# Products of a scan's keys: from two quarters of the PE array and one bank to four quarters and two banks

## The chip, the cores and the metric

The kernel runs on one core of a Trainium2 chip. The metric is the device time of one execution in microseconds (us). The engines are TensorE (PE in the rows; PEld is its weight load), VectorE (DVE), ScalarE (ACT), GpSimd (POOL) and SyncE (SP). SP only issues DMAs here; ScalarE issues DMAs too, in the same order as its other work. A quarter of the array is a 64x64 part of TensorE's 128x128 array: its rows are the partitions that the operands lie on, its columns the partitions of PSUM that the result goes to.

## The reference, cut to what matters

One layer of a diffusion backbone: a modulated input is projected to the columns of eight attention heads and of eight RWKV-7 heads with two directions; both go through an output projection, a norm and an MLP. What the change touches belongs to the RWKV-7 heads. The reference runs them as a recurrence:

```python
s_kk = jnp.einsum('bhij,bhj->bhi', S, kk_t)
S = (S * w_t[:, :, None, :] - s_kk[..., None] * (kk_t * a_t)[:, :, None, :]
     + v_t[..., None] * k_t[:, :, None, :])
return S, jnp.einsum('bhij,bhj->bhi', S, r_t)
```

The kernel computes it in chunks of 64 tokens. For each chunk, head and direction it needs a 64x64 matrix of products of decayed keys, which it then inverts as a triangular system.

## The kernel before, in words

The kernel has a first phase (`phase1`, to about 1000 us) and a second (`tail`). The first phase takes the 2304 tokens in three blocks of 768. For each block it projects the tokens to 27 groups of 128 columns (`project`, L450: 24 matmuls into a PSUM bank of the pool `psM`, which has two, emptied by ScalarE in L453). Between the halves of each projection `side` hands out one step of the other work, the scan terms among it.

The scan terms are made by `r1a` and `r1b`, 36 times each: three blocks, four pairs of heads (`p`), three groups of four chunks (`t`). `r1a` computes the decayed keys: `ar` and `bk`, two buffers each. They hold two heads on the halves of the 128 partitions, both directions (`d`), four chunks (`c`) and two kinds of vectors. The tile `ei` of `r1a` (written by the exponential in L646) has one buffer, which it shares, by its tag, with `lab` of `r1b`.

`r1b` stores `ar` and `bk` by SP's queue (L676 to L679). It then forms the key products (L686) for both heads, both directions and four chunks: 16 products of 64x64 by 64x64, all into one bank, `psl`, from the pool `psC`, which has two. ScalarE copies the bank to `lab` in one instruction (L688) and issues two stores to the DRAM tensor LB, one for each direction (L690). For all but the context tokens a matmul with a matrix of ones follows, the bonus sum (L693), into another bank of `psC`, which VectorE empties (L695). The pool `psC` also serves the transposes of values (L726) and of the inputs (L415).

Later `solve` reads LB back, inverts the matrices on VectorE (L760, L761) and joins the parts by 32x32 matmuls (L800). In the second phase the chunks are chained; there L1141 and L1145 form products of keys for each chunk with 64x64 weights, in two banks.

The program is written in the order of these calls, with a priority that falls in that order. A planner with its own model of times then orders the instructions of each engine: an instruction that is not ready by that model lets later ones go ahead, so that a burst of L686 stands within the matmuls of a projection. It also picks the buffers and puts in the semaphores. On the chip each engine keeps the planned order.

Of the kernel before, what the change touches and what calls it, by code (L numbers as in the profile page):

```python
# [8 lines left out]
F32 = mybir.dt.float32  # L9
# [52 lines left out]
class Kern:  # L62
# [604 lines left out]
    def r1b(self, sb, p, t, v, cell):  # L667
        nc = self.nc
        R = self.r1
        ctx = sb == 0 and t == 0  # L670
        s = slice(t * 256, t * 256 + 256)
        c0 = sb * 12 + t * 4
        ar, bk = cell["ar"], cell["bk"]
        w = 64 if ctx else 128
        for d in range(2):
            nc.sync.dma_start(self.AR[:, d, c0:c0 + 4, p, 0:w], ar[:, d].rearrange("p c x t -> p c (x t)")[:, :, 0:w])  # L676
            nc.sync.dma_start(self.BK[0:64, d, c0:c0 + 4, p, :], bk[0:64, d].rearrange("p c x t -> p c (x t)"))
            for x in range(2):
                nc.sync.dma_start(self.BK[64:128, d, c0:c0 + 4, p, (1 - x) * 64:(2 - x) * 64], bk[64:128, d, :, x, :])  # L679
        psl = self.psC.tile([128, 512], F32, name="psc")  # L680
        for d in range(2):
            for c in range(4):
                for hd in range(2):
                    hs = slice(hd * 64, hd * 64 + 64)
                    o = (d * 4 + c) * 64
                    nc.tensor.matmul(psl[hs, o:o + 64], lhsT=bk[hs, d, c, 0, :], rhs=ar[hs, d, c, 0, :], start=True, stop=True)  # L686
        lab = R.tile([128, 2, 4, 64], F32, tag="ei", name="lab")
        nc.scalar.copy(lab.rearrange("p d c t -> p (d c t)"), psl)  # L688
        for d in range(2):
            nc.scalar.dma_start(self.LB[:, d, c0 * 4 + p:(c0 + 3) * 4 + p + 1:4, :], lab[:, d])  # L690
        if not ctx:
            psb = self.psC.tile([128, 512], F32, name="psc")
            nc.tensor.matmul(psb[:, :256], lhsT=self.bones, rhs=cell["kds"], start=True, stop=True)  # L693
            bon = R.tile([128, 256], F32, tag="q1", name="bon", bufs=3)
            nc.vector.tensor_tensor(bon, psb[:, :256], v[:, s], ALU.mult)  # L695
            g = sb * 768 + t * 256 - 256
            nc.sync.dma_start(self.BON[p, :, g:g + 256], bon)
# [1235 lines left out]
```

## Time and profile before

| what | value |
|---|---|
| median of 3 runs | 3413.09 us (3408.29 to 3415.94) |
| the profiled execution's own time | 3414.7 us |
| its span, first to last instruction | 3412.9 us |
| mean granted TensorE clock | 0.968 |
| TensorE busy | 3192.8 us (94%) |
| VectorE busy | 2599.1 us (76%) |
| ScalarE busy | 1523.7 us (45%) |
| chain of waits, share of TensorE | 65% |

Busy times are those of one profiled execution; instructions that issue DMAs or handle semaphores are not counted as busy. A matmul's end is modelled: consecutive matmuls overlap in the records, so that the time for which a burst holds TensorE is read from its first start to the start of what follows. Each product in 32-bit floats shows as two instructions.

### The profile page before, as it was taken

Reading aid. Unit: us, or ns where it says so; the run is one execution under the profiler, and the core shown is the slowest. Engines: PE = TensorE matmul, PEld = TensorE weight load, DVE = VectorE, ACT = ScalarE, POOL = GpSimd, SP = SyncE. Lnnn points to the kernel's source line nnn. Section 1 sums busy time; section 2 is a strip of 40 time slices with the busy share of each in tenths; the row PEclk is TensorE's granted clock in tenths of the full one; section 3 lists DMA queues with packets and bytes.
Section 4 is the critical chain, followed back from the end, with each engine's and each line's share of the span. In section 5 each row is a group of like instructions: output and inputs, shape, how many; then the busy total and the mean of one; then the engine's idle time right before and its main releaser. Section 6 shows DMA issues by size and latency. Waiting matters only on the chain.

```text
span 3412.9 us, 65231 instructions
## 1 busy us (share of the span) xinstructions
PE 3192.8 (94%) x25176; PEld 2602.5 (76%) x25176; DVE 2599.1 (76%) x4907; ACT 1523.7 (45%) x2891; POOL 511.0 (15%) x535
## 2 busy tenths in 40 slices
PE   7999899899988899899979989999999989999998
PEld 3888888889876677677667767777788868888886
DVE  5567977888788778767768878866766657899778
ACT  4555465456535455454432124343433343337333
POOL 0000000000005454545343321000000000010001
PEclk9999999999989999999989989999999989999999
DMA  7487366826675655455374546666644455445441
GB/s 259 119 244 213 95 170 167 223 71 178 174 201 145 144 140 126 122 133 128 101 199 150 175 152 224 210 198 206 210 150 148 145 206 162 154 161 203 146 160 69
DMA packets 765338, 561.67 MB, mean 165 GB/s; under 512 B 380412, under 2 KB 653564, under 8 KB 763620
## 3 DMA queue, kind: packets, MB, share of 16 engines
q1 hardware_dynamic: 691738, 523.14, 52.0%
q10 hardware_dynamic: 73290, 34.37, 3.5%
q8 instruction: 198, 3.24, 0.4%
q14 instruction: 112, 0.92, 0.1%
HBM read 359.70 MB, written 197.66 MB: 163 GB/s over the span
## 4 chain that ended last, share of the span: by engine, by line
PE 65%; DVE 14%; DMA 11%; SPq 3%; issue 3%; ACT 2%; POOL 1%; ACTq 0%; DVEq 0%; POOLq 0%
PE psm L450 14%; PE psa L1530 8%; PE psqb L1728 7%; PE psqa L1728 7%; PE psb L1530 4%; PE ops L1346 4%; PE pse L1530 2%; PE psv L1051 2%; DMA ks<-AR 1%; PE psm L468 1%; DMA w<-in_mlp_w 1%; PE pst L1022 1%; PE psg L1141 1%; PE psl L986 1%; PE psd L117 1%
## 5 line engine op out<-in xcount | busy, mean ns | idle before, releaser
L450 PE MATMUL psm<-xh,wh 128*128 128x386 f32 (+1 forms) x1104 | 378.4, 345 | 17.4 <-DVE xh L420 9.5
L450 PE MATMUL psm<-xl,wh 128*128 128x386 f32 (+1 forms) x1104 | 378.8, 343 | 3.1 <-DVE xl L421 3.1
L450 PE MATMUL psm<-xh,wl 128*128 128x386 f32 (+1 forms) x1104 | 376.6, 341 | 0.0
L450 PEld LDWEIGHTS psm<-xh,wh 128*128 128x128 f32 x1104 | 209.2, 190 | 44.8 <-ACT row L453 15.1
L450 PEld LDWEIGHTS psm<-xl,wh 128*128 128x128 f32 x1104 | 209.5, 190 | 16.0 <-issue 8.0
L450 PEld LDWEIGHTS psm<-xh,wl 128*128 128x128 f32 x1104 | 208.8, 189 | 6.1 <-issue 4.1
L1530 PE MATMUL psa<-xh,w1h 128*128 128x512 f32 x512 | 203.9, 399 | 5.1 <-DVE p L1556 4.6
L1794 POOL TENSOR_TENSOR acc<-acc,g 128x1024 f32<-128x1024 f32 x8 | 28.9, 3641 | 1178.2 <-DVE acc L1737 1178.2
L1530 PE MATMUL psa<-xh,w1l 128*128 128x512 f32 x512 | 201.7, 394 | 2.5 <-DVE w1l L1461 2.5
L1530 PE MATMUL psa<-xl,w1h 128*128 128x512 f32 x512 | 202.3, 395 | 0.0
L1678 ACT CAST ah<-al 128x1024 fp32r<-128x1024 f32 x98 | 103.0, 1051 | 213.2 <-DMA al<-HU 205.1
L760 DVE TENSOR_TENSOR stmp<-mp,xp 128x1 f32<-128x1 f32 (+30 forms) x310 | 175.4, 566 | 22.7 <-DMA mp<-LB 10.3
L1679 DVE TENSOR_TENSOR al<-al,ah 128x1024 fp32r<-128x1024 f32 x98 | 121.3, 1237 | 86.0 <-ACT ah L1678 85.9
L436 DVE TENSOR_TENSOR wl<-wst,wh 128x1024 fp32r<-128x1024 f32 x81 | 98.8, 1220 | 98.5 <-ACT wh L435 85.8
L1461 ACT CAST w1h<-w1s 128x512 fp32r<-128x512 f32 x96 | 59.6, 621 | 226.4 <-DVE w1s L1450 87.4
L1728 PE MATMUL psqa<-uh,ah 128*128 128x512 f32 x400 | 155.8, 393 | 3.7 <-ACT uh L1634 3.2
L1728 PE MATMUL psqa<-ul,ah 128*128 128x512 f32 x400 | 157.4, 394 | 0.0
L1728 PE MATMUL psqa<-uh,al 128*128 128x512 f32 x400 | 157.0, 392 | 0.0
L1728 PE MATMUL psqb<-uh,ah 128*128 128x512 f32 x384 | 149.7, 393 | 7.5 <-ACT uh L1634 7.5
L761 DVE TENSOR_REDUCE xp<-stmp 128x1 f32<-128x1 f32 (+30 forms) x310 | 153.9, 497 | 3.1
L1728 PE MATMUL psqb<-ul,ah 128*128 128x512 f32 x384 | 151.0, 393 | 0.0
L1728 PE MATMUL psqb<-uh,al 128*128 128x512 f32 x384 | 150.6, 392 | 0.0
(393 smaller groups left out, 8816.2 us busy)
## 6 DMA issues: line engine op xcount, KB each, us to landing
al<-HU SPq DMA_DIRECT2D x106, 512.0 KB
wst<-in_w_in SPq DMA_DIRECT2D x81, 512.0 KB
w<-in_mlp_w SPq DMA_DIRECT2D x32, 1024.0 KB
wp<-in_mlp_w SPq DMA_DIRECT2D x32, 1024.0 KB
wmod<-in_w_mod SPq DMA_DIRECT2D x48, 512.0 KB
HU<-p SPq DMA_DIRECT2D x96, 256.0 KB
HU<-s SPq DMA_DIRECT2D x84, 256.0 KB
bkc<-BK SPq DMA_DIRECT2D x36, 512.0 KB
```

Of the source, the lines that this page charges most:

```text
L117: self.nc.tensor.matmul(acc[32 * j:32 * j + n, :], lhsT=self.sil[:, k, 0:n], rhs=w, start=(k == 0), stop=(k == 7))
L436: nc.vector.tensor_tensor(wl, w, f32(wh), ALU.subtract)
L450: nc.tensor.matmul(ps[:, :y - x], lhsT=s[:, k, :], rhs=m[:, k, x:y], start=(i == 0), stop=(i == 23))
L760: nc.vector.tensor_tensor(tv, mp[:, i:i + 1, lo:lo + n].to_broadcast([128, n, n]), xp[:, lo:lo + n, lo:lo + n], ALU.mult)
L761: nc.vector.tensor_reduce(xp[:, lo:lo + n, i], tv, AX.X, ALU.add)
L1051: nc.tensor.matmul(cell["ps"][hs, i0:i0 + n, :], lhsT=vt[:, hs], rhs=x, start=first, stop=last, skip_group_check=True)
L1346: nc.tensor.matmul(ps, lhsT=x[:, k, :], rhs=w[:, k, c], start=(i == 0), stop=(i == 23))
L1461: made[n] = nc.scalar.copy(h, x).ins, V.tensor_tensor(l, x, f32(h), ALU.subtract).ins
L1530: nc.tensor.matmul(ps, lhsT=w[:, k, :], rhs=x[:, k, :], start=(i == 0 and pr in (1, 5, 2)), stop=(i == 11), skip_group_check=True)
L1678: fs += [lambda: nc.scalar.copy(ah, f32(al)), fb[0], lambda: V.tensor_tensor(al, f32(al), f32(ah), ALU.subtract), fb[1]]
L1679: lambda: V.tensor_tensor(al, f32(al), f32(ah), ALU.subtract), fb[1]]
L1728: nc.tensor.matmul(ps, lhsT=x[:, c, s], rhs=y[:, c, :], start=(i == 0 and new), stop=(i == 5 and end), skip_group_check=True)
```

## The change

The 16 products of a call go to two banks, one for each direction. In direction 0 a head's result goes to the same half of the partitions as its operands; in direction 1 it goes to the other half. The loop over chunks is now outermost. ScalarE copies each bank by itself. Direction 0 is stored by one DMA; direction 1, whose halves lie swapped, by two, each of 64 partitions. LB holds the same as before.

```diff
-        psl = self.psC.tile([128, 512], F32, name="psc")
+        psl = [self.psC.tile([128, 4, 64], F32, name="psc") for _ in range(2)]
+        hs = [slice(0, 64), slice(64, 128)]
+        for c in range(4):
+            for d in range(2):
+                for h in range(2):
+                    nc.tensor.matmul(psl[d][hs[h ^ d], c, :], lhsT=bk[hs[h], d, c, 0, :], rhs=ar[hs[h], d, c, 0, :],
+                                     start=True, stop=True)
+        lab = R.tile([128, 2, 4, 64], F32, tag="ei", name="lab")
         for d in range(2):
-            for c in range(4):
-                for hd in range(2):
-                    hs = slice(hd * 64, hd * 64 + 64)
-                    o = (d * 4 + c) * 64
-                    nc.tensor.matmul(psl[hs, o:o + 64], lhsT=bk[hs, d, c, 0, :], rhs=ar[hs, d, c, 0, :], start=True, stop=True)
-        lab = R.tile([128, 2, 4, 64], F32, tag="ei", name="lab")
-        nc.scalar.copy(lab.rearrange("p d c t -> p (d c t)"), psl)
-        for d in range(2):
-            nc.scalar.dma_start(self.LB[:, d, c0 * 4 + p:(c0 + 3) * 4 + p + 1:4, :], lab[:, d])
+            nc.scalar.copy(lab[:, d], psl[d])
+        lb = self.LB[:, :, c0 * 4 + p:(c0 + 3) * 4 + p + 1:4, :]
+        nc.scalar.dma_start(lb[:, 0], lab[:, 0])
+        for h in range(2):
+            nc.scalar.dma_start(lb[hs[h], 1], lab[hs[1 - h], 1])
```

## Rows read from the trace of the kernel before

**Rows 1.** Busy time of each engine in three stretches, with granted clock and DMA.
```profile
160.00:270.00 110.00, 110.00 (x849) 89.71 (x849) 74.58 (x132) 63.24 (x129) 0.53 (x1) 1.00 0.85 239
270.00:372.00 102.00, 93.18 (x614) 81.40 (x610) 86.66 (x234) 54.23 (x99) 0.35 (x6) 0.95 0.70 192
...
700.00:1000.00 300.00, 291.20 (x2384) 265.43 (x2383) 243.80 (x438) 159.63 (x285) 3.97 (x5) 0.99 0.60 157
```
The columns of that view are the stretch, its length, the busy time and the number of instructions of PE, PEld, DVE, ACT and POOL, the granted clock, the DMA share and GB/s.

**Rows 2.** Chain of waits by line: 160 to 1000, 270 to 372, 700 to 1000.
```profile
by line: PE psm L450 48.2%; PE psm L468 5.6%; PE psc L686 3.5%; DMA xn<-in_x 2.6%; PE psb L614 2.1%; PE psb L624 1.7%; PE psd L117 1.7%; issue 1.6%; PE psb L628 1.6%; DMA LB<-lab 1.5%; PE psb L565 1.4%; PE psc L693 1.4%; DMA BK<-bk 1.4%; PE
...
by line: DMA xn<-in_x 11.4%; DMA BK<-bk 7.8%; DVE xl L421 6.5%; issue 6.0%; DMA Q<-rot 5.4%; DMA AR<-ar 5.1%; DVE xh L420 4.2%; DVE wl L436 3.9%; DMA KR<-rot 3.9%; DVE rsw L712 3.8%; DVE lst L202 3.7%; DVE cum L639 2.9%; DVE xn L373 2.8%; D
...
by line: PE psm L450 61.3%; PE psm L468 11.9%; PE psc L686 4.0%; PE psb L614 2.4%; PE psb L624 2.1%; PE psb L565 2.0%; PE psc L693 1.9%; PE psb L582 1.9%; PE psb L800 1.8%; PE psb L628 1.7%; SPq L775 1.6%; SPq L787 1.3%; PE psb L611 1.3%; D
```

**Rows 3.** The instructions of L686: count, duration in ns, first and last start.
```profile
L686 PE MATMUL psc<-ar,bk x1152: 218/218/365, 164.4 to 991.8; 64*64 64x64 f32 x192
L686 PEldq EVENT_SEMAPHORE  x26: 51/51/51, 162.2 to 987.6; - x26
```

**Rows 4.** Instructions in order of time: start us, us, engine, line; one burst.
```profile
829.57 1.15 PE L686 MATMUL psc<-ar,bk 64*64 64x64 f32 x32
...
830.65 0.70 PE L693 MATMUL psc<-kds,bones 128*128 128x256 f32 x2
```

**Rows 5.** In order of time, TensorE, second phase: L1145 alone, both, L1141 alone.
```profile
1279.80 0.68 PE L1145 MATMUL psg<-ks,bkc 64*64 64x64 f32 x16
...
1297.84 0.33 PE L1141 MATMUL psg<-ks,bkc 64*64 64x128 f32 x2
1297.86 0.33 PE L1145 MATMUL psg<-ks,bkc 64*64 64x64 f32 x4
...
1298.86 0.62 PE L989 MATMUL psx<-kc,qz 128*128 128x256 f32 x3
...
1303.07 1.09 PE L1141 MATMUL psg<-ks,bkc 64*64 64x128 f32 x16
```

**Rows 6.** In order of time, TensorE: the 32x32 matmuls of one solve.
```profile
448.78 1.29 PE L800 MATMUL psb<-svs,svx 32*32 32x32 f32 x128
```

**Rows 7.** ScalarE's groups, 160 to 1000 us: busy, mean ns, idle before.
```profile
L453 ACT COPY row<-psm 128x386 f32<-128x386 f32 (+1 forms) x119 | 55.6, 472 | 70.8 <-PE psm L450 62.5 <-DVE rot L714 2.5 <-PE psc L415 2.0
...
L688 ACT COPY lab<-psc 128x512 f32<-128x512 f32 x36 | 21.1, 585 | 41.1 <-PE psc L686 28.4 <-DVE bk L659 9.5 <-DVE rsw L715 3.1
```

**Rows 8.** Instructions of two lines of ScalarE: count, ns, first and last.
```profile
L616 ACT COPY vtok<-psb x36: 348/372/392, 150.5 to 980.6; 128x256 f32<-128x256 f32 x36
...
L690 ACTq DMA_DIRECT2D LB<-lab x72: 366/402/1500, 166.9 to 993.1; - x72
```

**Rows 9.** Who waited for whom, 160 to 1000 us: total, times, longest.
```profile
PE psm L450 <- ACT row L453: 7.7, 5, 3.2
...
PEld psm L450 <- ACT row L453: 12.5, 11, 3.4
...
ACT lab L688 <- PE psc L686: 28.4, 16, 5.8
...
ACT ei L646 <- DMA LB<-lab: 11.3, 10, 3.0
```

**Rows 10.** Chain of waits in order of time: start us, us, what.
```profile
269.79 1.10 PE psc L686 x32
...
303.69 2.39 DMA LB<-lab
...
600.36 5.39 DMA LB<-lab
```

**Rows 11.** In order of time: a burst, its late copy, its bonus sum.
```profile
484.48 1.15 PE L686 MATMUL psc<-ar,bk 64*64 64x64 f32 x32
...
488.94 0.60 ACT L688 COPY lab<-psc 128x512 f32<-128x512 f32 x1
...
489.74 0.59 PE L693 MATMUL psc<-kds,bones 128*128 128x256 f32 x2
```

## The prediction

> **What bounds the kernel now.** I read the page first, then the chain of waits, then the lines that the diff touches. By the page TensorE is busy for 94% of the span, but that is a mean over stages. The changed line runs only between 164 and 992 us [rows 3], in the first phase, so I cut that phase by what the chain passes through. From 160 to 270 and from 700 to 1000 us TensorE is busy for 110.00 of 110 and 291.20 of 300 us, at a granted clock of 1.00 and 0.99, the 2.4 GHz level; in between, from 270 to 372, it is busy for 93.18 of 102 us at 0.95 [rows 1]. The chain agrees: over 160 to 1000 us the line of the products, L686, holds 3.5% of it, 29.4 of 840 us; in 270 to 372 us the chain is DMAs and VectorE, and L686 is not among its first lines [rows 2]. One burst of 32 instructions takes 1.08 us, from 829.57 to the next start at 830.65 [rows 4], so 29.4 us are 27 of the 36 bursts. These 27 are where a shorter burst can move the end. The reader is to see that on the chain nothing is waited for at such a burst: the engine's other work stops, the burst runs, the other work goes on.
>
> **The products.** The 36 calls issue 1152 instructions, two for each of 16 products [rows 3]. All sixteen products of a call use two quarters of the array, head 0 the upper left and head 1 the lower right, so each quarter works off sixteen instructions in a row. After the change the first direction uses these two and the second direction the other two, with a bank of its own. No line of the first phase does that, but the scan in the second does: L1141 writes the two off-diagonal quarters of one bank, L1145 the two diagonal quarters of another, with 64x64 weights as here. Alone, 16 instructions of L1141 (128 columns) show 1.09 us and 16 of L1145 (64 columns) 0.68 us; 0.07 of each is a tail that runs beside the next instruction (a burst shows 1.15 and lets the next one start after 1.08 [rows 4]), so they hold the engine for 1.02 and 0.61 us. Issued in turns, both together hold it for 1.02 us, from 1297.84 to 1298.86 [rows 5]. The second pair of quarters is free beside the first. With 64 columns on both sides a burst should hold the engine as long as L1145 alone, 0.61 us. The gain is 0.47 us a burst; its ends are nothing (no overlap) and 0.54, half of 1.08. I take 0.47, since the row of both shows no cost of the second pair at all. On the chain that is 27 x 0.47 = 12.7 us less. The nine bursts off the chain are worth nothing; were all on the path, the gain would be 36 x 0.47 = 16.9 us.
>
> Two rules of the Trainium skill speak against this. In "TensorE: Matmul & The Clock Gate", section "The mechanism", it says that a weight load runs beside a matmul in flight only if it goes to another group of rows. The two products of one head now share their rows, so by this rule the burst would stay at 1.08 us. L1141 and L1145 share rows in the same way and do overlap [rows 5]. The same page, in the section "Wait — 56ns, not 53.3ns?", gives about 25 ns as the least time from start to start of matmuls; by that an estimate for 32 instructions is 0.80 us, 0.87 with the tail. In this trace 128 instructions of L800, in 32x32 tiles, show 1.29 us, about 10 ns each [rows 6], so the floor does not hold here.
>
> **The copies.** ScalarE's one copy of 512 columns takes 585 ns [rows 7]. Two of 256 columns take 2 x 372, by the copy L616 of that shape [rows 8]: 0.16 us more. They cannot start earlier, since the loop over chunks is outermost and both banks fill to the end. **The DMAs.** Three issues stand on ScalarE's queue in place of two, because the second direction lies with its halves swapped and each half is stored by itself. An issue costs that engine 0.40 us, from 0.37 to 1.50 [rows 8]. Together ScalarE has 0.56 us more in each call, 20 us in all. It is busy for 63.24 of 110 and 159.63 of 300 us [rows 1], so its throughput is no matter, only what stands in line behind.
>
> Two things do. First, the copied tile shares its one buffer with the next call's exponential (L646), which waits until the stores have landed: ten such waits, 11.3 us [rows 9]. On the chain I find three of these landings, from 2.39 to 5.39 us [rows 10]; each grows by 0.56 us: 1.7 us. Whether two stores of 64 partitions land later than one of 128 no row shows; the spread of the landings now gives the ends, 3.0 us less or more in each of the three, and I take no difference, since the bytes are the same. Second, projections wait for ScalarE to empty their bank (L453): 12.5 us in 11 waits and 7.7 in 5 [rows 9]. If all sixteen grew by 0.56 us it would be 9.0; there are 36 calls to 119 such copies [rows 7], so I take a quarter, 2.2. A gain is excluded here, since no work of ScalarE is taken away.
>
> **The banks.** The pool of these banks has two buffers. Before, a call took one for the products and one for the bonus sum (L693); now the products take both, and the bonus sum needs the first to be copied out. At 830.65 the sum directly follows the products [rows 4], and it does in nine calls. The order is the planner's; where it counts the copy as unfinished it puts projections ahead, as between 484.48 and 489.74, where the sum comes after the copy [rows 11]. I cost this at nothing, because that work covers it. If the cover is gone, all that TensorE has stands behind L693, the projections first, and the phase with them: from 0.47 us a time (a copy at once, 0.37, and the semaphores around it) to 3.7 (a copy that starts 3.3 us after the burst's end, as at 488.94 [rows 11]). A second bank to be claimed can also need one more semaphore instruction ahead of a burst, 51 ns [rows 3]: 27 x 0.05 = 1.4 us, with zero and double as ends.
>
> **Sum.** -12.7 + 1.7 + 2.2 + 1.4 = -7.4 us. The profiled execution took 3414.7 us, its span of 3412.9 and 1.8 around it, and would take 3407.3; from the median of three, 3413.09, the forecast is 3405.7.
>
> **Rivals.**
> Full gain: all 36 bursts count, and ScalarE's extra work falls into its idle time: 3413.1 - 16.9 = 3396.2. For it: ScalarE idles 41.1 us ahead of this copy alone [rows 7]. Against it: the stretch whose chain is not TensorE's [rows 2].
> Banks: the sum waits on the chip where the planner thought the copy done. It decides from about six uncovered sums on: nine at the mean of a free and a late ScalarE, (0.47 + 2.1) / 2 = 1.3 us each (2.1 is the middle of the two ends), cost 12, and the time is 3418, slower than before. For it: the copy comes late in 20 of 36 calls, since ScalarE waited for the products in 16 alone [rows 9]. Against it: the planner finds other work now wherever the sum cannot run [rows 11].
> Handed back: the stretches in the middle end by loads and VectorE whatever TensorE did before them, so only the bursts after 700 us count, 4.0% of 300 = 12.0 us [rows 2] or 11 bursts: 5.2 less and 5.3 more, 3413. Against it: the chain enters the stretch at 270 us through a burst [rows 10].
> No overlap, so that the change doesn't do what it says: the burst stays, and 0 + 5.3 gives 3418.4. The one row of four quarters speaks against it [rows 5]. This is what the rule on rows would do.
> A floor of issue: the burst goes to 0.87, so 27 x 0.21 = 5.7 less and 5.3 more, 3412.7. Against it stand the 10 ns of [rows 6]. This is what the rule of 25 ns would do.
>
> **Chances.** Forecast 0.51, full gain 0.15, banks 0.15, handed back 0.11, no overlap 0.05, floor 0.03. 0.2% of this time is 6.8 us, about what a measurement of this kernel can tell from no change. The forecast lies just beyond it; its own range is 3399 to 3410, and of its 0.51 I give 0.35 to faster and 0.16 to within. Faster: 0.35 + 0.15 = 0.50. Within: 0.16 + 0.11 + 0.05 + 0.03 = 0.35. Slower: 0.15. The range goes from a little under the full gain to the banks' case, 3394 to 3419.
>
> **What would show it.** A burst of 32 that holds TensorE for near 0.61 us shows the first step; 1.08 shows no overlap. Two copies near 0.37 us and three issues near 0.40 show the second. Idle time of TensorE before L693 that the copy ends shows the banks' rival. Waits of L646 for the stores of well over 11.3 us in all would show them to land later. The prediction is wrong if the bursts shrink by 0.47 us and the phase does not end some 7 us earlier, or if the second phase, whose code is the same, takes another time.

## The result, and the profile after

The kernel after took 3456.31 us (median of 4 runs, 3453.92 to 3459.0), the kernel before beside it 3410.69 (4 runs, 3402.93 to 3415.94): a ratio of 1.0133, 95% interval 1.0114 to 1.0152. It is slower by 1.3%, some 45 us, where 7 us less were forecast. The profiled execution of after has a span of 3456.4 us and a mean granted clock of 0.956 (0.968 before).

The edit did to TensorE what it was to do. One burst of after with its copies, stores and bonus sum, in order of time (start us, us, engine, line):

```profile
846.13 0.69 PE L687 MATMUL psc<-ar,bk 64*64 64x64 f32 x32
846.76 0.49 PE L614 MATMUL psb<-cmat,vx 128*128 128x128 f32 x2
846.86 0.65 ACT L691 COPY lab<-psc 128x256 f32<-128x256 f32 x2 [0.34 <-PE psc L687]
847.26 0.38 ACTq L693 DMA_DIRECT2D LB<-lab  x1
847.74 1.47 ACTq L695 DMA_DIRECT2D LB<-lab  x2
851.64 0.36 PEld L698 LDWEIGHTS psc<-kds,bones 128*128 128x128 f32 x2
```

The burst holds TensorE from 846.13 to 846.76: 0.63 us, where it was 1.08 [rows 4]. It does so in 28 of the 36 bursts (0.625 or 0.632 us); two are cut in half by other work, and in the other six something stands inside or TensorE idles behind. The rows of single lines (count, shortest, median and longest in ns, first and last start) are, for the semaphores of the burst, the copies, the whole store and the half stores of after:

```profile
L687 PEldq EVENT_SEMAPHORE  x30: 51/51/51, 159.8 to 1003.5; - x30
...
L691 ACT COPY lab<-psc x72: 350/374/396, 162.9 to 1007.7; 128x256 f32<-128x256 f32 x72
...
L693 ACTq DMA_DIRECT2D LB<-lab x36: 366/367/748, 163.5 to 1007.8; - x36
...
L695 ACTq DMA_DIRECT2D LB<-lab x72: 582/622/2260, 167.1 to 1009.0; - x72
```

A copy is what L616 said, 374 ns for 372 [rows 8]. A store of 64 partitions holds ScalarE's queue for 0.62 us, not for the 0.37 to 0.40 of a whole one [rows 8]. Who waited for whom in after, 160 to 1013 us (total, times, longest):

```profile
PE psc L415 <- DVE xn L373: 19.0, 6, 7.0
...
ACT ei L646 <- DMA LB<-lab: 13.0, 10, 3.8
...
PEld psm L450 <- ACT row L453: 8.0, 8, 3.6
...
PE psb L805 <- DMA svs<-XS: 7.4, 4, 3.8
...
PE psm L450 <- ACT row L453: 5.5, 4, 3.4
```

The waits that the prediction priced are no larger, or hardly: 13.0 for 11.3, and 8.0 and 5.5 for 12.5 and 7.7 [rows 9]. The bonus sum waits for the copy once, its weight load for 0.4 us. What is new on TensorE lies on lines that were not edited: transposes that wait for a normalised input (L415), and the solves' matmuls that wait for a load (L805, 7.4 us in 4; 2.5 in 3 before, as L800). L415 waited this little before:

```profile
PE psc L415 <- DVE xn L373: 5.4, 4, 2.8
```

ScalarE is held up too: its idle time that ends by the stores of LB, over all its lines, is 42.4 us in after and 16.7 in before. The time for issuing them, which does not count as busy, is in it.

The larger part of the loss lies where no line was changed. Two stretches of both kernels that hold the same work, the first phase and the second (stretch, its length, busy time and number of instructions of PE, PEld, DVE, ACT and POOL, granted clock, DMA share, GB/s), before and then after:

```profile
160.00:1000.00 840.00, 804.69 (x6317) 717.18 (x6315) 674.48 (x1313) 452.46 (x822) 7.37 (x20) 0.98 0.65 173
1015.00:1745.00 730.00, 662.39 (x9949) 521.78 (x9951) 544.01 (x1589) 357.48 (x961) 350.70 (x391) 0.96 0.54 129
```

```profile
160.00:1013.00 853.00, 796.12 (x6300) 706.14 (x6299) 674.01 (x1309) 452.65 (x853) 7.30 (x20) 0.95 0.63 169
1033.00:1789.00 756.00, 687.05 (x9879) 533.23 (x9880) 547.28 (x1578) 354.63 (x956) 348.66 (x391) 0.93 0.52 124
```

In the first phase TensorE is busy for 8.6 us less (804.69 - 796.12). The bursts alone are 14.9 us shorter (43.6 and 28.8 us of busy time), so its other work takes 6.3 us more, at a granted clock of 0.95 for 0.98. It is idle for 56.9 us in place of 35.3, and the stretch is 13 us longer. The second takes 26 us longer with the same instructions: TensorE is idle for 69.0 us, 67.6 before, but busy for 24.7 us more, at a granted clock of 0.93 in place of 0.96. By form: 512 transposes of the attention (L1022, then L1027) take 287 and 296 ns in the mean. First and last start of that line, before and after:

```profile
L1022 PE MATMUL pst<-ident,S x512: 270/273/476, 1024.3 to 1740.0; 128*128 128x128 f32 x171
```

```profile
L1027 PE MATMUL pst<-ident,S x512: 270/273/476, 1037.0 to 1786.5; 128*128 128x128 f32 x171
```

The line begins 12.7 us later and ends 46.5 us later; at the end of the spans it is 43.5 us (3456.4 and 3412.9). The two windows leave a few us out: from the last projection (996.2 and 1009.7 us) to the last of these transposes after takes 33 us longer. The chain of waits shows what the second phase follows; its first names before (1015 to 1745 us) and after (1033 to 1789):

```profile
by line: PE psv L1051 7.9%; DMA ks<-AR 6.5%; PE pst L1022 5.5%; PE psl L986 5.3%; DMA qz<-Q 4.7%; PE psg L1141 4.6%; issue 4.6%; PE psx L989 4.2%; DVE stmp L760 3.5%; DVE xp L761 3.0%; PE ry L1173 2.8%; PE us L1194 2.8%; PE ry L1184 2.5%; P
```

```profile
by line: DMA ks<-AR 7.8%; PE psv L1056 7.1%; DVE stmp L765 5.5%; PE psl L991 5.4%; PE psg L1146 5.3%; PE pst L1027 5.2%; PE psx L994 4.3%; DMA qz<-Q 4.3%; DVE xp L766 3.8%; DVE ks L1153 3.4%; issue 3.4%; PE ry L1178 3.0%; PE us L1193 2.8%; 
```

The chained scan's loads (ks), its solves (stmp) and its key products (psg) hold larger shares, the attention (psv) a smaller one. The orders of the two kernels part at the first call (TensorE's at 164.9 us of before) and differ on every engine behind it, not only around the products.

### The profile page after: what moved, and what is told of

Same layout as the page of the kernel before. It is cut to its first block, busy times and chain, and to the rows that moved or that the text cites. A ratio compares the mean times of both kernels' runs of the same rounds, so it can differ in the third digit from the quotient of the medians.

```text
span 3456.4 us, 65308 instructions
## 1 busy us (share of the span) xinstructions
PE 3212.3 (93%) x25176; PEld 2607.0 (75%) x25176; DVE 2608.8 (75%) x4907; ACT 1525.3 (44%) x2927; POOL 508.5 (15%) x535
## 4 chain that ended last, share of the span: by engine, by line
PE 64%; DVE 16%; DMA 11%; issue 3%; ACT 2%; SPq 2%; POOL 1%; ACTq 0%; DVEq 0%; POOLq 0%
PE psm L450 13%; PE psa L1535 8%; PE psqb L1733 7%; PE psqa L1733 7%; PE psb L1535 4%; PE ops L1351 3%; PE pse L1535 2%; DMA ks<-AR 2%; PE psv L1056 2%; PE psm L468 2%; PE psg L1146 1%; DVE stmp L765 1%; PE psl L991 1%; PE pst L1027 1%; PE psd L117 1%
## 5 line engine op out<-in xcount | busy, mean ns | idle before, releaser
L450 PE MATMUL psm<-xh,wh 128*128 128x386 f32 (+1 forms) x1104 | 379.7, 346 | 9.5 <-ACT row L453 5.5
L450 PE MATMUL psm<-xl,wh 128*128 128x386 f32 (+1 forms) x1104 | 379.8, 344 | 4.8 <-DVE xl L421 3.6
L450 PE MATMUL psm<-xh,wl 128*128 128x386 f32 (+1 forms) x1104 | 377.4, 342 | 0.0
L450 PEld LDWEIGHTS psm<-xh,wh 128*128 128x128 f32 x1104 | 209.9, 191 | 34.5 <-ACT row L453 11.4
L450 PEld LDWEIGHTS psm<-xl,wh 128*128 128x128 f32 x1104 | 210.5, 191 | 18.4 <-issue 8.0
L450 PEld LDWEIGHTS psm<-xh,wl 128*128 128x128 f32 x1104 | 209.7, 190 | 9.0 <-issue 7.5
```

The costliest lines, as they stand in the source:

```text
L450: nc.tensor.matmul(ps[:, :y - x], lhsT=s[:, k, :], rhs=m[:, k, x:y], start=(i == 0), stop=(i == 23))
```

## The experiments

The theory, after the result: the loss is the planner's. The edit changed the times that it plans with, and it ordered every engine anew, in both phases; the new order is worse. The rival: it is the change's own work (stores, copies, banks) that costs. To part the two, each engine was held to a given order: after the last instruction is made, every instruction of an engine is chained to the one that stands before it in a list, without a semaphore. The kernel before held to its own order is the same program, instruction for instruction.

```diff
     k.tail()
+    ordered(tc)   # each engine: list of instructions; each one is to follow the one before it in the list
```

All ratios are to the kernel before on the same chip.

| kernel | order | us, median | ratio | 95% interval |
|---|---|---|---|---|
| after | its own | 3456.31 | 1.0133 | 1.0114 to 1.0152 |
| after | second phase as before | 3431.17 | 1.0048 | 1.0034 to 1.0061 |
| after | as before | 3423.65 | 1.0016 | 1.0007 to 1.0026 |
| after | as before, bonus sum free | 3426.53 | 1.0027 | 1.0013 to 1.0041 |
| before | second phase as after | 3437.89 | 1.0067 | 1.0053 to 1.0081 |
| before, split store | as before | 3418.59 | 1.001 | 1.0 to 1.002 |
| after, whole store | as before | 3419.15 | 1.0011 | 1.0 to 1.0021 |
| after, turned by copies | as before | 3419.64 | 1.0012 | 1.0 to 1.0024 |
| the same, third bank | as before | 3413.79 | 0.9996 | 0.9984 to 1.0008 |
| the same, sum later | as before, 8 moves | 3414.64 | 0.9995 | 0.9983 to 1.0008 |
| new scheme in two thirds | as before | 3413.75 | 0.9989 | 0.9976 to 1.0002 |
| before, stores swapped | its own | 3437.61 | 1.0057 | 1.0038 to 1.0076 |
| before, split store | its own | 3429.91 | 1.0036 | 1.0022 to 1.0051 |

### First study: the order

**The change under the order of before.** Where before has one copy or two stores, after's two or three stand in their place.

> The changed kernel, with every engine's instructions held in the order that the planner gave the kernel before (issue-order edges alone; the two copies stand where the one stood, the three stores where the two stood). Theory 'plan': the shorter bursts gain as on the changed kernel's PE-bound stretches (12 bursts gave 6.5 us there) and the loss is the other order, so this runs at about 3405 us, 3398 to 3412; some of the 14 bonus sums that directly follow a burst may wait 0.5 us or more each for the first copy. Rival 'work': the two copies, the third store and the second bank cost the time themselves, so it stays near the changed kernel, 3440 to 3460.

Of 1.33% there remain 0.16% (5.5 us). So the order is most of the loss, and the work alone still gains nothing where 7 us were forecast. TensorE's waits in the first phase show one reason (160 to 1003 us):

```profile
ACT ei L646 <- DMA LB<-lab: 16.7, 11, 5.2
PEld psm L450 <- ACT row L453: 14.8, 10, 5.1
PEld psc L698 <- ACT lab L691: 14.6, 14, 3.8
PE psc L698 <- ACT lab L691: 12.5, 13, 3.7
PE psm L450 <- ACT row L453: 10.5, 4, 4.9
```

In the old order the bonus sum (L698) stands directly behind the burst in 13 of 32 calls, and now waits there for the copy, 12.5 us in 13 waits. That is the banks' rival, and it appears only because the order was held: in after's own order the sum stands there once. The stores show too; ScalarE in order of time in the same run:

```profile
192.03 0.63 ACT L691 COPY lab<-psc 128x256 f32<-128x256 f32 x2
...
193.15 0.37 ACTq L693 DMA_DIRECT2D LB<-lab  x1
193.61 2.65 ACTq L695 DMA_DIRECT2D LB<-lab  x2
196.75 0.38 ACTq L618 DMA_DIRECT2D VT<-vtok  x1
197.17 0.48 ACT L453 COPY row<-psm 128x386 f32<-128x386 f32 x1 [3.45 <-DMA LB<-lab]
```

The two half stores hold the queue for 2.65 us here, and a projection's evacuation stands behind them.

**The bonus sum left to the planner**, all else as before. `ordered` leaves L698 out of TensorE's list.

> As the kernel with all of the old order, but the bonus sum is left to the planner, which puts it 14 to 68 instructions behind the burst. Theory 'plan': 3400 us, 3394 to 3408, a few us less than with the sum directly behind the burst if that one waits for the copy. Rival 'work': 3440 to 3460.

1.0027, not told apart from 1.0016. The waits of L698 for the copy are gone, but the projections wait longer for L453 than in before (7.7 and 12.5 us [rows 9]):

```profile
PEld psm L450 <- ACT row L453: 23.1, 14, 5.5
PE psm L450 <- ACT row L453: 17.5, 8, 5.2
```

One wait took the place of the other.

**The second phase's order alone**, put on the change, and the other way round on the kernel before. The lists are cut to the instructions from `attn_init` on.

> The changed kernel, with the old order held in the second phase alone; the first phase is planned freely. Theory 'plan': the first phase loses its 13.6 us as in the changed kernel and the second phase takes what it took before, 3424 us, 3415 to 3435. Rival 'work': 3450 to 3460, since the second phase's loss of 31 us would come from the state that the first leaves, not from its own order.

> The kernel before, with the changed kernel's order held in the second phase alone. Nothing of the change's work is in it. Theory 'plan': the second phase loses about 31 us by its order, 3440 us, 3428 to 3450. Rival 'work': as before, 3405 to 3416.

With the old order in the second phase alone, after falls from 1.0133 to 1.0048. The kernel before, in which nothing of the change is done, goes to 1.0067 by after's order of the second phase. Its first phase is untouched (the last projection starts 1.8 us earlier than before), and its last attention transpose starts 24.3 us later. The second phase of that run:

```profile
1013.00:1769.00 756.00, 683.86 (x9938) 532.08 (x9938) 551.26 (x1583) 355.73 (x959) 349.13 (x391) 0.94 0.53 124
```

26 us longer than before, 21.5 of them TensorE's busy time, 4.5 idle, at a granted clock of 0.94 for 0.96: nearly the picture of after. How much of it the clock makes is not shown, and the mean clock alone does not make it: held to the old order, the kernel with the split store of the second study has 0.94 too, and a second phase only 2 us longer than before:

```profile
1018.00:1750.00 732.00, 666.18 (x9714) 524.38 (x9714) 544.03 (x1583) 355.97 (x957) 347.06 (x388) 0.94 0.54 127
```

The first large step of the kernel with after's second phase lies between 1240 and 1310 us. Its waits, its row of the same view, and the row of before up to the same place, as nearly as it can be told:

```profile
DVE stmp L760 <- DMA qz<-Q: 6.5, 1, 6.5
...
PE psg L1154 <- DVE stmp L760: 5.6, 1, 5.6
```

```profile
1240.00:1310.00 70.00, 59.68 (x914) 44.70 (x915) 42.62 (x139) 31.66 (x83) 29.71 (x35) 0.88 0.59 131
```

```profile
1240.00:1300.00 60.00, 56.24 (x957) 43.45 (x956) 39.16 (x138) 31.86 (x88) 28.62 (x35) 1.00 0.64 141
```

A solve's work on VectorE comes late, TensorE stands behind it at the scan's transposes for 5.6 us (1276.4 to 1282.1), and the granted clock of the stretch is 0.88, where before has 1.00. It is at the lower level, 1.2 GHz, from 1280.6 to 1287.3, in and after that wait, and again from 1297.7 to 1307.7, with no wait of over 0.8 us between 1287 and 1298 to go with it. The Trainium skill, "TensorE: Matmul & The Clock Gate", Part 1, says that activity releases the throttle and that the throttled state is the default; the first of the two falls agrees, the second is not explained here.

### Second study: what the change's work costs under a fixed order

**Only the third store.** The kernel before, old order:

```diff
+        nc.scalar.dma_start(lb[:, 0], lab[:, 0])
+        for h in range(2):
+            nc.scalar.dma_start(lb[h * 64:h * 64 + 64, 1], lab[h * 64:h * 64 + 64, 1])
```

> The kernel before, every engine held to its own planned order; only direction 1 is stored by two DMAs of 64 partitions in place of one of 128. No product is moved. Stores theory (the half stores hold ScalarE's queue 0.62 us each and take what the burst gives): about 0.88 us more of ScalarE in each of 36 calls, the projections and the next call's exponential wait for it, 4 to 12 us slower than before (ratio 1.001 to 1.0035). Banks theory (the bonus sum behind the burst waits for the first copy and takes the gain): no change, within 2 us. Nothing-to-gain theory (the first phase does not follow TensorE): no change, within 2 us.

3 us slower by the median, at the edge of what is told from none. The rows of its half stores repeat those of after (median 632 ns, 367 for the whole store of the same call), with one bank and one copy: the longer issue belongs to the 64 partitions.

**The change without the third store.**

```diff
+        for d in range(2):
+            nc.scalar.dma_start(lb[:, d], lab[:, d])
```

> The kernel after, held to the order of the kernel before, but direction 1 is stored by one whole DMA: its halves are left swapped in LB, so the second phase reads the wrong heads for that direction. Under the held order the unaltered change took 7 us more than before (ratio 1.0016). Stores theory: the third issue and the longer issue go, ScalarE has only 0.16 us more a call, 4 to 12 us come back, ratio 0.998 to 1.0005. Banks theory: nothing comes back, 1.0015, and the waits before the bonus sum stay near 12 us. Nothing-to-gain theory: 1.000 to 1.002.

1.0011 beside 1.0016: not told apart. ScalarE's idle time that ends by the stores of LB falls from 53.9 to 20.7 us, but the waits before the bonus sum stay:

```profile
PE psc L697 <- ACT lab L691: 13.9, 13, 3.5
```

The stores theory alone does not bring the gain back.

**Halves turned by copies, then with a third bank.**

```diff
+        psl = [self.psC.tile([128, 4, 64], F32, name="psc"),
+               self.psD.tile([128, 4, 64], F32, name="psd") if sb else self.psC.tile([128, 4, 64], F32, name="psc")]
...
+        nc.scalar.copy(lab[:, 0], psl[0])
+        for h in range(2):
+            nc.scalar.copy(lab[hs[h], 1], psl[1][hs[1 - h]])
```

> The kernel after, held to the order of the kernel before, with direction 1's halves put right by ScalarE: two copies of 64 partitions, each into the other half of the tile, and then two whole stores. A third copy of about 0.37 us takes the place of a third issue and of the two long ones. Stores theory: most of the gain of the run with one whole store, less 36 x 0.37 = 13 us of ScalarE of which a quarter or so counts: ratio 0.999 to 1.001. Banks theory: 1.0015 to 1.003, since the banks are read out later still. Nothing-to-gain theory: 1.000 to 1.002.

> As the run with the halves turned by copies, and direction 1's bank comes from the pool of one bank that the modulation used, in the two later thirds of the first phase (24 of 36 calls), so that there the bonus sum finds a free bank of its own as before. Banks theory: the waits of TensorE before the bonus sum fall from some 12 us to under 5, and the time falls by 5 to 10 us against the run without it, to 0.997 to 0.9995. Stores theory: within 3 us of the run without it. Nothing-to-gain theory: 1.000 to 1.002, with no wait left that could explain it.

Without the bank 1.0012, with it 0.9996: 6 us apart by the medians, though the intervals overlap. Set against each other, the two give 0.9983, 0.9971 to 0.9996 by an estimate from their 12 and 11 times, just clear of none. The waits that the bank removes, 12.5 us in 13 without it, are in the run with it:

```profile
PE psc L699 <- ACT lab L691: 7.2, 6, 3.6
```

All six stand in the first third, where the call has no third bank. In the two later thirds the burst's gain arrives: against before, the projections start 3.8 us late at 478 us and 1.8 at 551, four bursts later, and 2.8 late at 789 and 0.5 at 878, five bursts later. That is (2.0 + 2.3) / 9 = 0.48 us a burst, all that the burst was shortened by. Between these stretches it is given back: 1.8 late at 551, 2.7 at 700, with seven bursts between. (Each comes from one trace. Two traces with the same first phase, that of before and that of before with after's second phase, drift against each other by 0.2 us at most in the two stretches, and by up to 2.4 over the whole phase.)

### Third study: an edit that moves no work, and the two best versions

**Stores swapped.** The kernel before with its two stores in the other order, planned anew.

```diff
-        for d in range(2):
+        for d in (1, 0):
             nc.scalar.dma_start(self.LB[:, d, c0 * 4 + p:(c0 + 3) * 4 + p + 1:4, :], lab[:, d])
```

> The kernel before with one edit that moves no work: the two stores of a call are issued in the other order, direction 1 first. Nothing is held; the planner orders all anew, and its orders differ from those of before on every engine. Plan theory (the order that the planner happens to choose decides, whatever the edit): a ratio off 1 by more than 0.2%, anywhere from 0.996 to 1.015. Plan theory with a cause (the first solve of the second phase, which was planned behind the scan's first loads in the kernel after, costs the 25 us): this plan has that solve early as before, so 0.999 to 1.004. Rival (it is the change's own work that makes the plan bad): 0.999 to 1.001, and the second phase as long as before within 3 us.

1.0057: an edit that removes and adds no instruction costs 20 us. Its first phase ends 2 us late, its last attention transpose starts 22.8 us late. The second phase:

```profile
1018.00:1767.00 749.00, 669.90 (x9939) 524.53 (x9938) 551.91 (x1591) 357.62 (x961) 353.58 (x391) 0.95 0.53 126
```

19 us longer than before, 11.5 idle and 7.5 busy. The plan theory holds. The cause given with it does not: this plan issues the loads of the second phase's first solve (`mp`, from LB) ahead of the scan's first loads (`ks`), at 998.5 and 1016.9 us, as before has it (994.5 and 1013.3), and loses almost as much as the order of after, which has them behind (1061.7 and 1025.9).

**Split store, planned anew.** The edit of the second study without the lists.

> The kernel before with direction 1 stored by two DMAs of 64 partitions, now ordered by the planner itself; under the order of before it took 0.1% more. Plan theory: off that by more than 0.2% either way. With the cause (this plan has the first solve of the second phase late, behind the scan's first loads, as the kernel after has): the second phase 20 to 30 us longer, ratio 1.006 to 1.011. Rival (the change's own work): 1.000 to 1.002.

1.0036, where the same program under the old order took 1.001. Its second phase is 11 us longer than before, not the 20 to 30 that the cause asked for. This plan has three of the solve's four loads late and by the medians loses 8 us less than the last one, which had them early (hardly told apart): against the cause again. One thing goes with the loss in all four kernels whose second phase is long: the first solve's work on VectorE starts 43.9 to 45.6 us behind the scan's first load, and 39.9 us in before. No run moves that alone. Which place in the order makes the second phase long stays open.

**The bonus sum later, in the first third.** The version with the third bank; in TensorE's list eight sums stand up to 20 instructions later.

> The run with halves turned by copies and a third bank, held to the order of before, but in TensorE's order the eight bonus sums of the first third stand up to 20 instructions later, so that projections cover the copy there too. Banks theory: the 7.2 us of TensorE's waits before the bonus sum in 160 to 372 us fall under 2, the first phase ends 3 to 7 us earlier than in that run, ratio to before 0.9975 to 0.999. Nothing-to-gain theory (the stretches between the thirds end by other engines): 0.999 to 1.0005, the waits gone but the end of the phase where it was.

Its waits for the copy are gone from 160 to 1003 us, but the time is the same, 0.9995 for 0.9996. The last projections start 1.2 us earlier than before, 0.8 in the run without the move. That run's trace is ahead of before by 3.0 us already at 156 us, this one by 0.7, so that by single traces the move gives 2.6 us in the phase, at the edge of their drift. By the time, the nothing-to-gain theory was right.

**The new scheme in the two later thirds only.**

```diff
+        quarters = [(c, d, h) for c in range(4) for d in range(2) for h in range(2)] if sb else [
+            (c, d, h) for d in range(2) for c in range(4) for h in range(2)]
```

> The first third of the calls (12 of 36) is computed as before, the other 24 with four quarters, two banks (one from the pool of the modulation) and the halves turned by copies; held to the order of before. Banks theory: nothing is lost in the first third, 24 bursts give back what they gave in the run with the third bank between 483 and 986 us, 4.2 us: 3 to 6 us faster than before, ratio 0.998 to 0.9992. Nothing-to-gain theory: 0.9995 to 1.0005.

0.9989, interval 0.9976 to 1.0002. Its first phase by the first and last projection, before and then in this run:

```profile
L450 PE MATMUL psm<-xh,wh x1104: 277/339/688, 48.1 to 996.2; 128*128 128x386 f32 x169, 128*128 128x258 f32 x15
```

```profile
L450 PE MATMUL psm<-xh,wh x1104: 277/339/688, 47.3 to 991.6; 128*128 128x386 f32 x169, 128*128 128x258 f32 x15
```

The last one starts 4.6 us earlier than before (4.1 without the 0.5 that the trace is ahead by at 156 us), near the 4.2 that were expected, of 24 x 0.46 = 11 us that the bursts were shortened by. This is the fastest version, over 1% faster than after by the ratios, but not told from the kernel before.

## Why the prediction was wrong

**The burst was right.** 0.63 us for 0.61, by the rows of L1141 and L1145. The rule on weight loads of the Trainium skill ("TensorE: Matmul & The Clock Gate", "The mechanism") does not describe these products: the two of one head share their rows, and the burst is at 0.63 us, not at 1.08. Nor does the 25 ns of the same page: 32 instructions in 0.63 us are 20 ns each.

**The step that failed is the one on the banks and the order**: "The order is the planner's; where it counts the copy as unfinished it puts projections ahead ... I cost this at nothing, because that work covers it." As far as it goes this held: in after the sum waits for the copy once, for 0.4 us. But the planner does not shift one instruction and leave the rest. By the runs the new order costs 0.85% in the second phase (1.0133 against 1.0048) and 0.32% in the first (1.0048 against 1.0016), about 29 and 11 us; put on the kernel before, the second phase's order costs 0.67%, 23 us. The sum had no term for it and the range no case. The prediction named its own refutation, "if the second phase, whose code is the same, takes another time", and priced that at nothing. The swapped stores, which add and remove no work, cost 0.57%, and the split ones 0.36% when planned anew against 0.10% under the old order: some 20 and 9 us, beside a sum of -7.4 and a largest term of 12.7. All three new orders are slower than that of before; whether one can also be faster no run shows, nor which place in the order costs the time.

**The gain of 12.7 us was too large also without the new order.** Under the old order the work alone is at 1.0016, 5.5 us slower, so 13 us off the -7.4. With a third bank, whole stores and old order it is at 0.9996. TensorE's busy time did fall there, from 804.69 to 791.97 us in 160 to 1000 (that this is 12.7 us, the forecast term, is chance: all 36 bursts count in it), but the phase ends only 0.8 us earlier, and the time went into idling. In the run of two thirds, 4.6 of 11 us reach the end of the phase. So 27 bursts on the chain do not mean 27 gains. The chain between the thirds was loads, stores and VectorE (270 to 372 us [rows 2]; in 560 to 700 TensorE's projections, L450, hold 7.7% of it, where they hold 76.9% in 372 to 560), and those stretches take back what came before, by the starts of the projections above. That is the kind of the rival "handed back", to which I gave 0.11.

**The half stores were mis-sized.** "An issue costs that engine 0.40 us" was read from whole stores. 64-partition stores stood in the trace before, on SP's queue (L677, median 584 ns), and were not looked at. ScalarE has 0.81 us more a call for issues, not 0.40 (0.37 + 2 x 0.62 against 2 x 0.40), and 1.0 us with the copies, not 0.56. By itself this costs about 3 us (1.001), at the edge of what is told from none.

**The other terms.** The waits of L646 for landed stores grew by 1.7 us in after (13.0 for 11.3). That this is the forecast term is luck: it meant three landings on the chain, this is all ten waits, and under the old order they grew by 5.4. For the evacuations the sum had 2.2 more; they fell in after and grew under the old order by 2.8 for TensorE and 2.3 for its weight loads (10.5 for 7.7, 14.8 for 12.5), where the order does not move away from them. The semaphore of the burst is there 30 times in place of 26 [rows 3], 0.2 us at 51 ns each, where 1.4 were put down.

**Two readings.** The bonus sum directly follows the burst in 13 calls of before, not nine: four more do so across a gap or with other work inside the burst. And the floor's rival set 0.87 us, with the tail, against 1.08, without it; like against like is 0.80, and the rival's time 3411. Neither changes the forecast.

## What to carry to other kernels

Where a planner orders the instructions, an edit is two changes: its work and a new order of everything, and the second has to be priced too. A null edit, such as two stores swapped, shows what size it can have; holding the order shows the work. And a burst that stands on the chain is worth its time only as far as the next stretch that ends by something else.

## What was not expected of the hardware

A store of 64 partitions to LB holds ScalarE's queue for longer than one of 128, 0.62 us against 0.37, and up to 2.26. ScalarE copies 64 partitions into the other half as fast as 128 in place: 368 ns and 372 for 256 columns in the run of two thirds:

```profile
L690 ACT COPY lab<-psc x24: 352/372/386, 474.8 to 987.5; 128x256 f32<-128x256 f32 x24
L692 ACT COPY lab<-psd x48: 363/368/372, 475.2 to 988.2; 64x256 f32<-64x256 f32 x48
```

The same instructions of the second phase took TensorE 662 to 667 us of busy time in the ten traces with the order of before, at granted clocks of 0.94 to 0.96; 669 and 670 with the orders of the split and the swapped stores, planned anew (0.96 and 0.95); 684 with after's order behind the old first phase (0.94), 687 behind after's own (0.93). The order goes with the busy time; the mean clock does not sort it.
